# Input projection of a hybrid encoder block: 512-column token-major products, and q, k, v of two heads accumulated while x arrives

## The chip, the cores and the metric

The kernel runs on one core of a Trainium2 chip. The metric is the device time of one launch in microseconds (us). TensorE (PE) multiplies, VectorE (DVE), ScalarE (ACT) and GpSimd (POOL) do elementwise work, and DMA queues move data between DRAM, the on-chip SBUF and, by the engines, PSUM, where TensorE accumulates. P is 128.

## The reference, cut to what matters

One layer on x of 1024 tokens by 1024 features, all fp32. The change concerns the first lines, the input projection of 3104 columns, and what feeds on it.

```python
h = rms_norm(x, norm_mix)                     # x * rsqrt(mean(x*x) + eps) * gain
proj = h @ w_in                               # 1024 x 3104
q, k, v, z, b_f, b_b, a_f, a_b, su, sv = split(proj, [512, 512, 512, 512, 8, 8, 8, 8, 512, 512])
qkv = silu(short_conv(concat(q, k, v), conv_w))           # 5 taps along the tokens
o_a = bidir_gated_deltanet(qkv, z, b_f, b_b, a_f, a_b)    # 8 heads of 64, chunks of 64 tokens, two directions
o_b = spatial_gating(su, sv)                  # gelu, rms norm of v, a 128x128 mix of the tokens of a chunk, u * mix, rms norm
x = x + concat(o_a, o_b) @ w_out
x = rms_norm(x + square(relu(rms_norm(x) @ w_ff1)) @ w_ff2)
```

The rms factor of a token (1/rms) is one number per token. The kernel multiplies with the gain-scaled x and applies the factor to the products.

## The kernel before

*Precision.* Each fp32 operand is split into a rounded part and a remainder (xh and xl, w[:, 0] and w[:, 1]), and `mm3` makes one product from three matmuls (L140 to L142): first high by high, then the two cross terms. A `PE` line L140 in the profile is thus any large product; the tiles tell which.

*First stage (`first`).* For each of the 8 slices dt of 128 features, x comes transposed (xT, 512 KB), ACT and DVE make xh and xl, and eight blocks of 128 tokens accumulate 288 columns in eight PSUM banks: half of z and the 32 gate columns. Then x is read a second time, token by token (xtok), and ACT sums its squares (L241). POOL raises to the power -0.5 (`rsqrt`, L134 and L135). The result per token, rstd, is transposed on TensorE (L250) and written to DRAM as rs_d (L253), and read back over all partitions as rrow (L254): channel-major products, which have tokens along the columns, need a row.

*Projection (`project`).* Items follow each other in the order "01z23abcd". A digit is a head pair: q, k and v, each 128 channels by two halves of 512 tokens, with w stationary and x moving (channel-major). z is the other half of z, and a to d are the four gating groups, with x stationary and 256 columns of w moving (token-major, `tok_mm`). An item's weights are loaded while the one ahead runs: SP reads 512 KB into raw, ACT casts it (L148), POOL subtracts (L149). There are three such w buffers and two raw buffers.

*After an item.* A channel-major half is multiplied by rrow on DVE into cx (L330); then come the five-tap convolution on DVE and ACT (L422 to L428), turns to token order on TensorE (L450), the products of chunks (`stage1`: L548 in 64x64 tiles), an inversion of 32x32 triangles on DVE (L579, L581; L589 and L591 transpose its result into V and VT), and products of 32x32 tiles (L599, L611, L612). Decay factors are made by L517. The token-major parts go through ACT (gelu L337, silu L265) to `sgu`, which mixes four token blocks of one group at a time.

*Order.* `run` is a planner: each step is a generator that yields its cost ("pe 2.6 act 1" means 2.6 us of PE and 1 of ACT), lanes ("conv", "chunk0", "sgu", ...) queue such steps, and a lane's step is put in front of the projection's next when the planner's clocks of the engines say that it is ready by then. The clocks begin at the values of `self.t.update(dve=2.0, act=4.0, pool=3.0)`. What it gives out is one program; a scheduler then orders each engine's queue, where chunk, scan and convolution steps carry a priority. Engines run their queues in order.

*Then* come the scan (L743 to L810) with the out-projection, and the MLP of 3072 matmuls of 512 columns.

Of the kernel before, what the change touches and what calls it, by code (L numbers as in the profile page):

```python
# [10 lines left out]
F32 = mybir.dt.float32  # L11
# [8 lines left out]
P = 128  # L20
S = 1024
# [32 lines left out]
class Kern:  # L54
# [149 lines left out]
    def tok_mm(self, ps, b, w, dts):  # L204

        tb = slice(b * P, (b + 1) * P)
        for dt in dts:
            wd = w[dt // 4]
            self.mm3(ps, self.xh[dt][:, tb], self.xl[dt][:, tb], wd[:, 0, dt % 4], wd[:, 1, dt % 4],
                     dt == 0, dt == NT - 1)  # L210

    def first(self, xp):

        nc, a, tkx, tkp = self.nc, self.a, self.tkx, self.tkp
        N = 288
# [3 lines left out]
        acc = [self.psd() for _ in range(3)] + [self.psg() for _ in range(5)]  # L219
        two = [tkx.tile([P, 2, S], F32, tag=k, name="xraw") for k in ("n", "A")]  # L220
        one = lambda: self.rawp.tile([P, S], F32, tag="raw", name="xraw")
        w = []
        for dt in range(NT):
            if dt in (0, 1, 4, 7):
                k = 1 if dt in (0, 7) else 3
                pool, tag = {0: (self.wp, "w"), 1: (self.wp, "w"), 4: (tkx, "cm"), 7: (tkp, "lane")}[dt]
                raw = self.cvp.tile([P, k, N], F32, tag="ca", name="raw", bufs=2)
                t = self.load_w(a["wz1"][:, dt:dt + k], raw, pool.tile([P, 2, k, N], F32R, tag=tag, name="w"), nc.gpsimd)
                w += [t[:, :, i] for i in range(k)]
            self.load_x(dt, xp, two[dt // 2 - 1][:, dt % 2] if 2 <= dt < 6 else one())  # L230
            if dt == 0:
                self.late_consts()
            for b in range(NB):
                tb = slice(b * P, (b + 1) * P)
                self.mm3(acc[b][:, :N], self.xh[dt][:, tb], self.xl[dt][:, tb], w[dt][:, 0], w[dt][:, 1],
                         dt == 0, dt == NT - 1)
        for b in range(NB):
            xr = (tkx, "tok") if b % 2 else (self.cvp, "cx")
            xr = xr[0].tile([P, D], F32, tag=xr[1], name="xtok", bufs=2)
            nc.sync.dma_start(xr, a["x"][b])  # L240
            nc.scalar.activation(xr, xr, AF.Square, accum_out=ss[:, b:b + 1])  # L241
        self.w0 = self.load_in(a["wqkv"][0], [NT, P])
        raw = tkp.tile([P, 3, N], F32, tag="nod", name="raw")
        for b in range(3):
            (nc.scalar.copy if b == 1 else nc.vector.tensor_copy)(raw[:, b], acc[b][:, :N])
            acc[b] = raw[:, b]
        with self.tc.high_priority(offset=400):
            self.rsqrt(self.rstd, ss, 1.0 / D)
# [5 lines left out]
            nc.sync.dma_start(self.rrow, self.rs_d.partition_broadcast(P))  # L254
        gt = tmp[:, 0:256].rearrange("p (b c) -> p b c", b=NB)
        for b in range(NB):
            nc.vector.tensor_scalar(gt[:, b], acc[b][:, 256:288], self.rstd[:, b:b + 1], None, ALU.mult)
            self.evac_z(acc[b], b, 1)
        return gt, tmp, sml

    def evac_z(self, ps, b, h):
        nc = self.nc
        if b % 4 == 0:
            self.zt = self.sgup.tile([P, 4, 256], F32, tag="uv", name="zt", bufs=3)
        nc.scalar.activation(self.zt[:, b % 4], ps[:, 0:256], AF.Silu, scale=self.rstd[:, b:b + 1])  # L265
        if b % 4 == 3:
            nc.sync.dma_start(self.z_d[b - 3:b + 1, :, h * 256:h * 256 + 256].rearrange("b t c -> t b c"), self.zt)

    def project(self):
# [3 lines left out]
        qkv = lambda p: [("q", p, j) for j in range(3)]  # L273
        items = []
        for c in "01z23abcd":
            items += qkv(int(c)) if c.isdigit() else [("z", 0, 0)] if c == "z" else [("s", "abcd".index(c), 0)]

        def load(kind, p, j):
            if kind == "q":
                return self.load_in(self.a["wqkv"][p * 3 + j], [NT, P])  # L280
            return [self.load_in(self.a["ws"][p, h] if kind == "s" else self.a["wz0"][h], [4, 256]) for h in range(2)]
# [6 lines left out]
        w = self.w0  # L288
        for it, (kind, p, j) in enumerate(items):
            nxt = None  # L290
            if kind == "q":
                n = p * 3 + j - 2
                yield lambda: n < 0 or n in self.taps
                for h in range(2):
                    yield "pe 2.6" + (" act 1 pool 2.3" if h else "")
                    if h == 0:
                        x = self.cvp.tile([P, S + 4], F32, tag="cx", name="cx", bufs=2)
                        nc.gpsimd.memset(x[:, 0:2], 0.0)
                        nc.gpsimd.memset(x[:, S + 2:S + 4], 0.0)
                    else:  # L300
                        nxt = load(*items[it + 1])
                    ps = self.psd()
                    th = slice(h * 512, h * 512 + 512)
                    for dt in range(NT):
                        if dt == NT // 2:
                            yield "pe 2.6 dve .6"
                        self.mm3(ps, w[:, 0, dt], w[:, 1, dt], self.xh[dt][:, th], self.xl[dt][:, th],
# [3 lines left out]
            else:  # L311
                for h in range(2):
                    if kind == "s":
                        yield lambda: self.uv > 0
                    for i in range(4):
                        yield "pe 2.6 act .4" + (" act 1 pool 2.3" if h and i == 1 else "")
                        if i == 0 and kind == "s":
                            self.uv -= 1
                            uv = self.sgup.tile([P, 4, 256], F32, tag="uv", name="uv", bufs=3)
                        if h and i == 1 and it + 1 < len(items):  # L320
                            nxt = load(*items[it + 1])
                        ps = self.psd()
                        self.tok_mm(ps[:, :256], h * 4 + i, w, range(NT))
                        late.append((self.evac_sgu, ps, uv, i, p, h) if kind == "s" else (self.evac_z, ps, h * 4 + i, 0))
                        flush(1)
# [9 lines left out]
    def evac_sgu(self, ps, uv, i, g, h):  # L335
        b = h * 4 + i
# [873 lines left out]
```

## Time and profile before

| what | us |
| --- | --- |
| median of 3 runs (lowest, highest) | 1381.99 (1380.45, 1386.76) |
| the profiled execution | 1388.61 |
| its span on the core | 1386.6 |
| PE busy / DVE / ACT / POOL | 1333.1 / 734.8 / 499.8 / 255.1 |
| first stage, projection, scan and out-projection, MLP | to 37.6, to 412, to 687, to the end |

The span is what the trace covers; 2.0 us of the execution lie around it. Shares of busy time are averages over stages. A matmul's busy time is modelled, so its pitch, the distance from start to start in a stretch, says more than its mean duration. PEclk is the clock that was granted to TensorE, as a share of the full one.

### The profile page before, as it was taken

What the parts mean: (1) busy time and instruction counts of PE and PEld (TensorE: products, weight loads), DVE (VectorE), ACT (ScalarE), POOL (GpSimd) and SP (SyncE); (2) the same over time, 40 slices, a digit from 0 to 9 for tenths busy, and PEclk for the clock granted to TensorE, in tenths of its full rate; (3) what the DMA queues carried; (4) which work ended last, traced back from release to release, by engine and by line L of the source; (5) the groups of instructions that cost most, each with busy time, mean ns of one, the idle gap of its engine ahead of it and who ended that gap; (6) DMA issues with size and microseconds to landing.
All of it is one profiled execution on the core that took longest, in us unless ns stands there. A gap on an engine that the chain in (4) does not pass through costs nothing.

```text
span 1386.6 us, 21359 instructions
## 1 busy us (share of the span) xinstructions
PE 1333.1 (96%) x8606; PEld 1124.1 (81%) x8606; DVE 734.8 (53%) x1201; ACT 499.8 (36%) x924; POOL 255.1 (18%) x330
## 2 busy tenths in 40 slices
PE   7899999999987999998999999999999999999997
PEld 7677876889987898876788888888888888888885
DVE  3579677976664566686543433434334343343345
ACT  5565443574545663411531311312113121131224
POOL 2232212233365875100000000000000000000013
PEclk9999899989989999999999999999999999999999
DMA  9622232235235563320012102121021210212103
GB/s 335 246 97 109 93 85 78 85 100 160 80 65 138 131 158 80 117 77 1 1 54 69 42 12 69 54 69 38 16 69 54 69 38 16 69 54 69 36 18 129
DMA packets 125617, 113.55 MB, mean 82 GB/s; under 512 B 75048, under 2 KB 98736, under 8 KB 124976
## 3 DMA queue, kind: packets, MB, share of 16 engines
q1 hardware_dynamic: 124368, 110.10, 25.4%
q10 hardware_dynamic: 1152, 2.10, 0.4%
q8 instruction: 68, 1.11, 0.3%
q14 instruction: 29, 0.24, 0.1%
HBM read 85.42 MB, written 27.33 MB: 81 GB/s over the span
## 4 chain that ended last, share of the span: by engine, by line
PE 78%; DVE 11%; ACT 3%; POOL 2%; issue 2%; DMA 2%; SPq 1%; POOLq 0%; ACTq 0%; DVEq 0%
PE psd L140 14%; PE psd L141 14%; PE psd L142 13%; PE psg L140 9%; PE psg L141 9%; PE psg L142 9%; PE psg L752 3%; DVE lt L579 2%; DVE lane L581 2%; PE psg L548 2%; PE psg L743 2%; PE pss L797 1%; DVE ca L425 1%; DVE cm L425 1%; PE psg L599 1%
## 5 line engine op out<-in xcount | busy, mean ns | idle before, releaser
L140 PE MATMUL psg<-fh,w 128*128 128x512 f32 x512 | 199.3, 389 | 0.6 <-DVE fl L964 0.6
L142 PE MATMUL psd<-w,ff 128*128 128x512 f32 x512 | 199.3, 389 | 0.0
L141 PE MATMUL psd<-w,ff 128*128 128x512 f32 x512 | 199.2, 389 | 0.0
L141 PE MATMUL psg<-fl,w 128*128 128x512 f32 x512 | 199.1, 389 | 0.0
L142 PE MATMUL psg<-fh,w 128*128 128x512 f32 x512 | 198.0, 389 | 0.0
L148 ACT CAST w<-raw 128x512 fp32r<-128x512 f32 (+3 forms) x122 | 98.8, 811 | 268.7 <-PE psd L142 150.0
L140 PE MATMUL psd<-w,ff 128*128 128x512 f32 x512 | 195.3, 389 | 0.0
L1038 DVE SCALAR_TENSOR_TENSOR x<-psd,r,x 128x512 f32<-128x512 f32 x128 | 94.5, 749 | 170.0 <-PE psd L142 169.9
L149 DVE TENSOR_TENSOR w<-raw,w 128x512 fp32r<-128x512 f32 (+1 forms) x96 | 83.4, 870 | 103.7 <-ACT w L148 101.8
L996 POOL TENSOR_SCALAR fs<-fs 128x1 f32<-128x1 f32 x8 | 5.5, 693 | 671.8 <-ACT scr L993 671.8
L1021 ACT ACTIVATE relu<-psg 128x512 f32<-128x512 f32 x64 | 38.1, 595 | 244.7 <-PE psg L142 244.7
L140 PEld LDWEIGHTS psg<-fh,w 128*128 128x128 f32 x512 | 96.1, 188 | 20.8 <-DVE fl L964 0.8
L140 PEld LDWEIGHTS psd<-w,ff 128*128 128x128 f32 x512 | 96.1, 188 | 20.3 <-DVE x L1038 0.4
L141 PEld LDWEIGHTS psd<-w,ff 128*128 128x128 f32 x512 | 96.2, 188 | 20.0
L142 PEld LDWEIGHTS psg<-fh,w 128*128 128x128 f32 x512 | 96.1, 188 | 20.0
L141 PEld LDWEIGHTS psg<-fl,w 128*128 128x128 f32 x512 | 96.1, 188 | 19.9
L142 PEld LDWEIGHTS psd<-w,ff 128*128 128x128 f32 x512 | 96.1, 188 | 20.0
L140 PE MATMUL psd<-w,xh 128*128 128x256 f32 (+1 forms) x344 | 104.0, 305 | 7.9 <-ACT xh L199 7.9
L1022 DVE TENSOR_TENSOR relu<-relu 128x512 f32<-128x512 f32 x64 | 44.2, 690 | 115.1 <-ACT relu L1021 115.1
L141 PE MATMUL psd<-w,xh 128*128 128x256 f32 (+1 forms) x344 | 102.8, 302 | 0.0
L142 PE MATMUL psd<-w,xl 128*128 128x256 f32 (+1 forms) x344 | 101.6, 301 | 0.0
L140 PE MATMUL psd<-xh,w 128*128 128x512 f32 x192 | 77.6, 404 | 3.0 <-DVE cx L330 2.6
(229 smaller groups left out, 2523.0 us busy)
## 6 DMA issues: line engine op xcount, KB each, us to landing
raw<-in_w SPq DMA_DIRECT2D x32, 512.0 KB, 3.6
raw<-in_w SPq DMA_DIRECT2D x64, 256.0 KB, 2.5
raw<-in_wqkv SPq DMA_DIRECT2D x12, 512.0 KB, 3.5
tok_d<-tok SPq DMA_DIRECT2D x12, 512.0 KB, 4.7
xtok<-in_x SPq DMA_DIRECT2D x8, 512.0 KB
t_d<-zero SPq DMA_DIRECT2D x8, 512.0 KB, 7.6
a_d<-A SPq DMA_DIRECT2D x4, 1024.0 KB, 3.9
raw<-in_ws SPq DMA_DIRECT2D x8, 512.0 KB, 3.5
```

Source lines behind the costliest of these rows:

```text
L140: mm(ps, lh, rh, start=start, stop=False)
L141: mm(ps, lh, rl, start=False, stop=False)
L142: mm(ps, ll, rh, start=False, stop=stop)
L148: nc.scalar.copy(w[:, 0], raw)
L149: lo.tensor_tensor(w[:, 1], raw, w[:, 0].bitcast(F32), ALU.subtract)
L425: nc.vector.scalar_tensor_tensor(acc, x[:, t:t + S], cw[:, t:t + 1], acc, ALU.mult, ALU.add)
L548: nc.tensor.matmul(ps[c * 64:c * 64 + 64, b * 64:b * 64 + 64], cm[1][hs, ch], cm[w][hs, ch], start=True, stop=True)
L579: nc.vector.tensor_tensor(tv, X[:, k:k + 1, 0:k].broadcast_to([P, m, k]), X[:, k + 1:32, k:k + 1].broadcast_to([P, m, k]), ALU.mult)
L752: nc.tensor.matmul(ps[:, (r * 2 + t) * P:(r * 2 + t + 1) * P], l[:, r, t], uw[:, r, t], start=True, stop=True)
L1021: nc.scalar.activation(r, pf, AF.Relu)
L1022: nc.vector.tensor_tensor(r, r, r, ALU.mult)
L1038: nc.vector.scalar_tensor_tensor(x1[b][:, ns], pf, r4[:, b:b + 1], x1[b][:, ns], ALU.mult, ALU.add)
```

## The change

- The first stage accumulates q, k and v of head pair 0 (six banks of 512 columns, channel-major, 18 matmuls for each dt) and the gates alone (one bank, 32 columns for a token block, L253 after). Its weights w0 are 416 columns wide: three times 128 and 32.
- x is not read again: ACT squares the xT slices, DVE adds them up, and eight matmuls against a column of ones (L258) give the sums per token. rstd (L262) is laid on diagonals (dg) on DVE, and two matmuls of ones by dg (L270) give rrow in PSUM, which ACT copies. rs_d is gone.
- z is one item of 512 columns, and the gating groups go two at a time, 256 columns of u and 256 of v: order "z1a23b". `sgu` works on two token blocks of two groups instead of four blocks of one.
- Weights come in pieces of 512 columns with nine buffers. Those of the first stage are made as before. Of the others ACT writes the rounded part and its negative, and a DMA from POOL's queue adds the fp32 weights onto the negative (`accum_op`, L164).
- The squares of q, k and of sgu go to a PSUM tile; the token-order tile `tok` is one tile of two halves with a write for each half; one convolution buffer is moved (cax); the planner's clocks begin at dve=0, act=6.

The diff, cut to its core:

```diff
-    def load_in(self, src, shape):
-        raw = self.rawp.tile([P] + shape, F32, tag="raw", name="raw")
-        w = self.wp.tile([P, 2] + shape, F32R, tag="w", name="w")
-        return self.load_w(src, raw, w, self.nc.gpsimd)
+    def piece(self, src, n=512, early=False):
+
+
+        nc = self.nc
+        raw = self.rawp.tile([P, 512], F32, tag="raw", name="raw")[:, :n]
+        w = self.wp.tile([P, 2, 512], F32R, tag="w", name="w")
+        if early:
+            self.load_w(src, raw, w[:, :, :n], nc.gpsimd)
+        else:
+            nc.sync.dma_start(raw, src)
+            nc.scalar.copy(w[:, 0, :n], raw)
+            nc.scalar.mul(w[:, 1, :n], raw, -1.0)
+            nc.gpsimd.dma_start(w[:, 1, :n], src, accum_op=ALU.add)
+        return w
...
+            w.append(self.piece(a["w0"][dt], N, True))
+            self.load_x(dt, xp, xraw[dt])
+            pool, tag = (tkx, "cax") if dt % 2 else (self.cvp, "ca")
+            sq = sqs if dt == 0 else pool.tile([P, S], F32, tag=tag, name="sq")
+            nc.scalar.activation(sq, xraw[dt], AF.Square)
+            if dt:
+                nc.vector.tensor_tensor(sqs, sqs, sq, ALU.add)
...
+        self.w0 = [self.piece(a["wt"][0, dt]) for dt in range(NT)]
+        for dt in range(NT):
+            for i in range(6):
+                j, h = divmod(i, 2)
+                ws, th = slice(j * P, j * P + P), slice(h * 512, h * 512 + 512)
+                self.mm3(qkv[i], w[dt][:, 0, ws], w[dt][:, 1, ws], self.xh[dt][:, th], self.xl[dt][:, th],
+                         dt == 0, dt == NT - 1)
             for b in range(NB):
-                tb = slice(b * P, (b + 1) * P)
-                self.mm3(acc[b][:, :N], self.xh[dt][:, tb], self.xl[dt][:, tb], w[dt][:, 0], w[dt][:, 1],
-                         dt == 0, dt == NT - 1)
-        for b in range(NB):
-            xr = (tkx, "tok") if b % 2 else (self.cvp, "cx")
-            xr = xr[0].tile([P, D], F32, tag=xr[1], name="xtok", bufs=2)
-            nc.sync.dma_start(xr, a["x"][b])
-            nc.scalar.activation(xr, xr, AF.Square, accum_out=ss[:, b:b + 1])
-        self.w0 = self.load_in(a["wqkv"][0], [NT, P])
-        raw = tkp.tile([P, 3, N], F32, tag="nod", name="raw")
-        for b in range(3):
-            (nc.scalar.copy if b == 1 else nc.vector.tensor_copy)(raw[:, b], acc[b][:, :N])
-            acc[b] = raw[:, b]
-        with self.tc.high_priority(offset=400):
-            self.rsqrt(self.rstd, ss, 1.0 / D)
-            rst = self.psd()
-            nc.tensor.transpose(rst[:NB, :P], self.rstd, self.ident)
-            rsr = sml[:NB, 128:256]
-            nc.vector.tensor_copy(rsr, rst[:NB, :P])
-            nc.sync.dma_start(self.rs_d.rearrange("(b t) -> b t", t=P), rsr)
-            nc.sync.dma_start(self.rrow, self.rs_d.partition_broadcast(P))
+                tb, gs = slice(b * P, (b + 1) * P), slice(3 * P, N)
+                ps = gate[:, b * 32:b * 32 + 32]
+                for i, (x, k) in enumerate(((self.xh, 0), (self.xh, 1), (self.xl, 0))):
+                    nc.tensor.matmul(ps, x[dt][:, tb], w[dt][:, k, gs], start=dt == b == i == 0, stop=dt == NT - 1 and i == 2,
+                                     skip_group_check=True)
+            if dt == NT - 3:
+
+                for b in range(NB):
+                    nc.tensor.matmul(gate[:, 256 + b:257 + b], sqs[:, b * P:(b + 1) * P], ones[:, 0:1],
+                                     start=False, stop=True, skip_group_check=True)
+                with self.tc.high_priority(offset=400):
+                    nc.vector.tensor_scalar(ss, gate[:, 256:256 + NB], 1.0 / D, EPS, ALU.mult, ALU.add)
+                    nc.gpsimd.tensor_tensor(self.rstd, ss, self.mhalf.broadcast_to([P, NB]), ALU.pow)
+
+                    dg = self.sgup.tile([P, NB, P], F32, tag="uv", name="dg", bufs=3)
+                    nc.vector.tensor_tensor(dg, self.ident.unsqueeze(1).broadcast_to([P, NB, P]),
+                                            self.rstd.unsqueeze(2).broadcast_to([P, NB, P]), ALU.mult)
+            if dt == NT - 2:
+                with self.tc.high_priority(offset=100):
+                    for h in range(2):
+                        nc.tensor.matmul(misc, ones, dg[:, h * 4:h * 4 + 4].rearrange("p b t -> p (b t)"),
+                                         start=True, stop=True)
+                        nc.scalar.copy(self.rrow[:, h * 512:h * 512 + 512], misc)
...
-        for c in "01z23abcd":
...
+        for c in "z1a23b":
...
+            for _ in range(min(n, len(todo))):
+                nxt.append(self.piece(todo.pop(0)))
...
+                    ps = self.psd()
+                    tb = slice(b * P, (b + 1) * P)
+                    for dt in range(NT):
+                        if dt % 4 == 0:
+                            yield "pe 2.7 act .3" + (" act 1.2" if b >= 6 and dt == 0 and todo else "")
+                        if b >= 6 and dt == 0:
+                            load(1)
+                        self.mm3(ps, self.xh[dt][:, tb], self.xl[dt][:, tb], w[dt][:, 0], w[dt][:, 1], dt == 0, dt == NT - 1)
...
-                sq = self.sgup.tile([P, 512], F32, tag="sj", name="sq")
+                sq = self.psg()
...
-        nc.sync.dma_start(self.tok_d[p, j], tok.rearrange("p b c -> p (b c)"))
+            nc.sync.dma_start(self.tok_d[p, j][:, h * 512:h * 512 + 512], tok)
...
-        self.mm3(pm, ws[:, 0, g], ws[:, 1, g], vs[:, 0].rearrange("p b c -> p (b c)"),
-                 vs[:, 1].rearrange("p b c -> p (b c)"), True, True)
+        for g in range(2):
+            self.mm3(pm[:, g * 256:g * 256 + 256], ws[:, 0, k * 2 + g], ws[:, 1, k * 2 + g], vh[:, :, gs[g]],
+                     vl[:, :, gs[g]], True, True)
...
-        self.wp = self.pool("wp", 3, right, **R)
+        self.wp = self.pool("wp", 9, right, **R)
...
-        self.t.update(dve=2.0, act=4.0, pool=3.0)
+        self.t.update(dve=0.0, act=6.0, pool=3.0)
```

What it moves on the engines, at three places. On TensorE in the projection, the products of a chunk (`stage1`, 64x64 tiles; L548 before, L590 after) stood one by one between the 256-column products of z. Before:

```order
L548 MATMUL psg<-ca 64x64 x25
L140 MATMUL psd<-w,xh_227 128x256
L548 MATMUL psg<-ca 64x64
L141 MATMUL psd<-w,xh_227 128x256
L548 MATMUL psg<-ca 64x64
L142 MATMUL psd<-w,xl_228 128x256
L548 MATMUL psg<-ca 64x64
L140 MATMUL psd<-w,xh_261 128x256
```

After, pair 0's stand among pair 1's 512-column products:

```order
L559 MATMUL psg<-dr_650,dl 128x512 x3
L590 MATMUL psg<-ca,cm 64x64 x16
L590 MATMUL psg<-cm 64x64 x2
L493 MATMUL psg<-cst,cm 128x128 x4
L590 MATMUL psg<-cm 64x64 x14
L140 MATMUL psd<-xh_201,w 128x512
L141 MATMUL psd<-xl_202,w 128x512
L142 MATMUL psd<-xh_201,w 128x512
```

They now stand in blocks. (The number behind ` x` is a count; a row's tile names are output<-inputs.) Up to the first product of the scan, TensorE goes to 64x64 tiles and back 64 times before and 15 times after, to 32x32 tiles 17 and 18 times; after, 17 times it goes from 32x32 to 64x64 tiles, where pair 1's L653 and L654 (L611 and L612 before) alternate with L590.

On TensorE in the first stage, in the stretch of one dt. Before:

```order
L140 MATMUL psd<-w,xh_169 128x288 x3
L140 MATMUL psg<-w,xh_169 128x288 x5
L141 MATMUL psd<-w,xh_169 128x288 x3
L141 MATMUL psg<-w,xh_169 128x288 x5
L142 MATMUL psd<-w,xl_170 128x288 x3
L142 MATMUL psg<-w,xl_170 128x288 x5
```

After, a part of one dt:

```order
L140 MATMUL psg<-xh_175,w 128x512
L141 MATMUL psg<-xl_176,w 128x512
L142 MATMUL psg<-xh_175,w 128x512
L253 MATMUL psg<-w,xh_175 128x32 x2
L253 MATMUL psg<-w,xl_176 128x32
L253 MATMUL psg<-w,xh_175 128x32 x2
L253 MATMUL psg<-w,xl_176 128x32
```

24 products of 288 columns have become 18 of 512 and 24 of 32.

On POOL, from the first weights to the first qkv item's. Before:

```order
L149 TENSOR_TENSOR w<-raw,w 128x1024
L298 MEMSET cx 128x2
L299 MEMSET cx 128x2
L134 TENSOR_SCALAR sml<-sml 128x8
L135 TENSOR_TENSOR rstd<-sml,mhalf 128x8
L149 TENSOR_TENSOR sgw<-raw,sgw 128x512
L495 MEMSET zero 128x1024
L149 TENSOR_TENSOR w<-raw,w 128x1024 x2
```

After:

```order
L149 TENSOR_TENSOR w<-raw,w 128x416 x8
L164 DMA w<-in_wt 128x512 x7
L262 TENSOR_TENSOR rstd<-sml,mhalf 128x8
L149 TENSOR_TENSOR sgw<-raw,sgw 128x512
L164 DMA w<-in_wt 128x512
L164 DMA w<-in_wqkv 128x512
L537 MEMSET zero 128x1024
```

The subtractions of whole items have become DMA issues, and seven of them, for z's weights, stand ahead of rstd.

More of the change, by code (lines that the diff above doesn't have):

```diff
@@ L218, in first @@
         ss = sml[:, 0:NB]
-        acc = [self.psd() for _ in range(3)] + [self.psg() for _ in range(5)]
-        two = [tkx.tile([P, 2, S], F32, tag=k, name="xraw") for k in ("n", "A")]
-        one = lambda: self.rawp.tile([P, S], F32, tag="raw", name="xraw")
+        qkv = [self.psd(), self.psd()]
+        misc = self.psd()
+        qkv += [self.psg() for _ in range(4)]
+        gate = self.psg()
+        two = [tkx.tile([P, 2, S], F32, tag=k, name="xraw") for k in ("n", "A", "cm")]
+        xraw = [t[:, i] for t in two for i in range(2)] + [tkp.tile([P, S], F32, tag=k, name="xraw") for k in ("lane", "nod")]
@@ L222, in first @@
+        ones = self.sgup.tile([P, P], F32, tag="sm", name="ones", bufs=2)
+        nc.vector.memset(ones, 1.0)
+        sqs = self.sgup.tile([P, S], F32, tag="uv", name="sqs", bufs=3)
         w = []
         for dt in range(NT):
[L224 to L229, printed above, removed]
@@ L262, in evac_z @@
         nc = self.nc
[L263 to L267, printed above, removed]
+        if b % 2 == 0:
+            self.zt = self.sgup.tile([P, 2, 512], F32, tag="uv", name="zt", bufs=3)
+        nc.scalar.activation(self.zt[:, b % 2], ps, AF.Silu, scale=self.rstd[:, b:b + 1])
@@ L269, in project, with new_cx, third @@
+        if b % 2:
+            nc.sync.dma_start(self.z_d[b - 1:b + 1].rearrange("b t c -> t b c"), self.zt)
+    def new_cx(self):
+        x = self.cvp.tile([P, S + 4], F32, tag="cx", name="cx", bufs=2)
+        self.nc.gpsimd.memset(x[:, 0:2], 0.0)
+        self.nc.gpsimd.memset(x[:, S + 2:S + 4], 0.0)
+        return x
+    def third(self):
+        yield "dve 1.4"
+        x = self.new_cx()
+        for h in range(2):
+            self.evac_qkv(self.qkv0[4 + h], x, h, 0, 2)
     def project(self):
@@ L286, in flush, with load @@
                 f(*args)
-        w = self.w0
+        for j in range(2):
+            yield "dve 1.4"
+            x = self.new_cx()
+            for h in range(2):
+                self.evac_qkv(self.qkv0[j * 2 + h], x, h, 0, j)
+        self.side("conv", self.third())
+        w, todo = self.w0, []
+        def load(n):
+            for _ in range(min(n, len(todo))):
+                nxt.append(self.piece(todo.pop(0)))
         for it, (kind, p, j) in enumerate(items):
-            nxt = None
+            nxt = []
+            after = loads(*items[it + 1]) if it + 1 < len(items) else []
             if kind == "q":
@@ L293, in project @@
                 yield lambda: n < 0 or n in self.taps
+                todo = after
                 for h in range(2):
-                    yield "pe 2.6" + (" act 1 pool 2.3" if h else "")
+                    yield "pe 2.6" + (" act 2.4" if todo else "")
+                    load(4 - h)
                     if h == 0:
[L297 to L301, printed above, removed]
+                        x = self.new_cx()
                     ps = self.psd()
@@ L311, in project @@
             else:
-                for h in range(2):
-                    if kind == "s":
-                        yield lambda: self.uv > 0
[L315 to L325, printed above, removed]
+                load(len(todo))
+                w += nxt
+                nxt, todo = [], after
+                for b in range(NB):
+                    if kind != "z" and b % 2 == 0:
+                        yield lambda: self.uv > 0
+                        self.uv -= 1
+                        uv = self.sgup.tile([P, 2, 512], F32, tag="uv", name="uv", bufs=3)
+                    ps = self.psd()
[6 more added lines that the diff above has]
+                        self.mm3(ps, self.xh[dt][:, tb], self.xl[dt][:, tb], w[dt][:, 0], w[dt][:, 1], dt == 0, dt == NT - 1)
+                    late.append((self.evac_z, ps, b) if kind == "z" else (self.evac_sgu, ps, uv, b, "ab".index(kind)))
+                    flush(1)
             w = nxt
@@ L444, in heads @@
             yield "pe .5 " + ("act 1.1 dve .6" if j < 2 else "dve .7")
-            if h == 0:
-                tok = self.tkx.tile([P, NB, P], F32, tag="tok", name="tok", bufs=2)
-                self.opened += 1
+            tok = self.tok[:, h]
             pt = self.psg()
@@ L492, in zeros @@
     def zeros(self):
-        z = self.sgup.tile([P, 4, 256], F32, tag="uv", name="zero", bufs=3)
+        z = self.sgup.tile([P, 2, 512], F32, tag="uv", name="zero", bufs=3)
         self.nc.gpsimd.memset(z, 0.0)
@@ L889, in outproj @@
         t = [tkx.tile([P, 2, D], F32, tag=k, name="x1") for k in ("cm", "n", "A")]
-        self.x1 = [t[b // 2][:, b % 2] for b in range(6)] + [tkx.tile([P, D], F32, tag="tok", name="x1", bufs=2) for _ in range(2)]
+        self.x1 = [t[b // 2][:, b % 2] for b in range(6)] + [tkx.tile([P, D], F32, tag=k, name="x1") for k in ("tok", "cax")]
         for b in range(NB):
@@ L1046, in scratch @@
         self.z_d = dp.tile([NB, P, 512], F32, name="z_d")
-        self.rs_d = dp.tile([S], F32, name="rs_d")
         self.cg_d = dp.tile([2, 16, 2, 2, 8, 64], F32, name="cg_d")
```

103 lines of the change are left out of this document (50 added, 53 removed).

## The prediction

> **What bounds the kernel now.** I read the page first (busy shares, slices, the chain that ended last), then TensorE in four stretches, then its waits and its timeline.
>
> ```profile
> span 1386.6 us, 21359 instructions
> PE 1333.1 (96%) x8606; PEld 1124.1 (81%) x8606; DVE 734.8 (53%) x1201; ACT 499.8 (36%) x924; POOL 255.1 (18%) x330
> ...
> PEclk9999899989989999999999999999999999999999
> ...
> PE 78%; DVE 11%; ACT 3%; POOL 2%; issue 2%; DMA 2%; SPq 1%; POOLq 0%; ACTq 0%; DVEq 0%
> ```
>
> ```profile
> 0.00:37.60 37.60, 29.61 (x193) 0.95 0.90 318
> 37.60:412.00 374.40, 355.54 (x3210) 0.93 0.34 109
> 412.00:687.00 275.00, 257.90 (x2179) 0.98 0.34 90
> 687.00:1386.00 699.00, 690.01 (x3042) 1.00 0.15 52
> ```
>
> The columns after a stretch's length are TensorE's busy time with its instructions, its granted clock, the DMA share and GB/s. TensorE is the bound throughout. The MLP (last row) runs at full clock with 9 us of idle time and isn't edited. The projection (second row) has 374.4 - 355.5 = 18.9 us of idle time and a clock of 0.93, worth up to 0.07 x 374.4 = 26 us. Busy time is not work here, though: a matmul that waits for the array counts as busy. That shows in the timeline, where 64x64 products alternate with wide ones (columns: start, duration, line, shapes, count):
>
> ```profile
> 128.58 0.34 PE L548 MATMUL psg<-ca 64*64 64x64 f32 x6
> 128.85 0.38 PE L140 MATMUL psd<-w,xh 128*128 128x256 f32 x1
> 129.17 0.32 PE L548 MATMUL psg<-ca 64*64 64x64 f32 x2
> 129.42 0.38 PE L141 MATMUL psd<-w,xh 128*128 128x256 f32 x1
> ...
> 219.32 0.50 PE L142 MATMUL psd<-xh,w 128*128 128x512 f32 x1
> 219.76 0.33 PE L548 MATMUL psg<-cm,ca 64*64 64x64 f32 x2
> 220.01 0.50 PE L140 MATMUL psd<-xh,w 128*128 128x512 f32 x1
> ```
>
> One wide and two small take 129.42 - 128.85 = 0.57 us, or 220.01 - 219.32 = 0.69. The pitches of undisturbed stretches come from windows (the first busy column is TensorE):
>
> ```profile
> 18.21:34.16 15.95, 15.95 (x123) 15.95 (x122) 5.74 (x4) 10.73 (x16) 4.00 (x5) 1.00 1.03 383
> 71.73:89.10 17.37, 17.37 (x78) 14.36 (x77) 14.57 (x12) 6.48 (x9) 6.73 (x6) 1.00 0.30 90
> 160.47:169.18 8.71, 8.71 (x76) 8.71 (x74) 5.17 (x13) 6.07 (x8) 4.05 (x6) 1.00 0.16 63
> ```
>
> The order has 76 matmuls of 512 columns in the second and 72 of 256 in the third (the rest overlap its edges): 0.2286 and 0.121 us each. The first has about 120 of 288 columns: 0.1325. The small ones cost 0.27/6 = 0.045 at most, so one round trip between tile sizes costs 0.57 - 0.12 - 0.09 = 0.36 us and 0.69 - 0.23 - 0.09 = 0.37 us. The Trainium skill ("TensorEngine Tiling (Array Packing)", Key Properties) says that changing the tiling mode drains TensorE; it gives no price, and these rows agree with the rule. The clock falls in just such stretches, of small or alternating products:
>
> ```profile
> 130.00:150.00 20.00, 20.00 (x78) 0.57 0.20 80
> 400.00:412.00 12.00, 11.14 (x234) 0.61 0.54 105
> ```
>
> **The change, part by part.** *First stage.* Before: 192 matmuls of 288 columns and one transpose, 37.6 us. After: 18 x 8 = 144 of 512 columns, 144 x 0.2286 = 32.9 us, and 192 gate products of 32 columns, each with its own 128-column weight load. No row has these; the nearest are 64 columns wide:
>
> ```profile
> 64.69 0.55 PE L377 MATMUL psg<-tmp,sums 128*128 128x64 f32 x4
> 65.08 1.05 PE L381 MATMUL psg<-tmp,sums 128*128 128x64 f32 x8
> 65.94 0.48 PE L141 MATMUL psd<-xl,w 128*128 128x512 f32 x1
> ```
>
> (65.94 - 65.08)/8 = 0.108 us, so 192 x 0.108 = 20.6 us; the lower bound is the 0.045 above (8.6 us), the upper the 0.1325 of 288 columns (25.4 us). I take 20.6, since the width is nearest. The eight ones-matmuls for the sums add 8 x 0.108 = 0.9 us, and the two plain fp32 ones of 512 columns 2 x 8 x 0.108 = 1.7, an estimate that scales those 64 columns by eight. The start, 37.6 - 29.6 = 8.0 us of idle time, and some 4 us of slow first matmuls (29.6 against 192 x 0.1325 = 25.4) stay. 56.1 + 8 + 4 = 68 us at most, 64 if the wait for data in the middle is covered by longer matmuls; I take 66: **+28 us**.
>
> *Projection columns.* Before, after the first stage: 576 matmuls of 512 columns (131.7 us) and 960 of 256 (116.2 us). After: 432 + 576 of 512, 1008 x 0.2286 = 230.4 us. **-17.5 us**. With the first stage, **+10.5**: the wider columns save 12 us and the gates, no longer part of a wide matmul, cost about 20.
>
> *Tile-size trips.* Counted in the two orders up to the first scan product: before 64 trips between 128 and 64 and 17 between 128 and 32; after 15 and 18, and 17 between 64 and 32, since L590's blocks stand together. 81 x 0.37 = 30 us before; after 33 x 0.37 = 12, and 17 for 0 to 6 (nothing in the trace shows a 32/64 trip; I take 3). **-15 us** (-12 to -18).
>
> *The rms row.* Before, L253 and L254 write and read it through DRAM behind 4 MB of zeros, and x is read a second time (8 x 512 KB).
>
> ```profile
> 45.82 0.45 SPq L498 DMA_DIRECT2D t_d<-zero  x1
> ...
> 48.66 1.14 SPq L254 DMA_DIRECT2D rrow<-rs_d  x1
> 49.84 7.80 SPq L498 DMA_DIRECT2D t_d<-zero  x6
> ```
>
> ```profile
> PE psg L599 <- DVE VT L591: 5.2, 2, 4.4
> PE psd L140 <- DVE cx L330: 2.6, 1, 2.6
> ...
> PE psd L142 <- POOL w L149: 1.7, 1, 1.7
> ```
>
> In this list of TensorE's waits (total, times, longest), the row's lateness costs 2.6 us and the POOL subtraction 1.7 us; both go. Late next is the pair-0 evacuation (L330, six at 0.685 us on DVE) and the last z weights, which get a buffer only when TensorE frees it; 2 us come back.
>
> ```profile
> L330 DVE TENSOR_TENSOR cx<-psd,rrow 128x512 f32<-128x512 f32 x24 | 16.2, 685 | 4.2 <-PE psd L142 4.2
> ```
>
> L599's waits for DVE's transposes stay: the DVE work of a pair is the same. I take idle **-5 us**: 18.9 to 14 (5 to 25).
>
> *Clock.* The worst interleaved stretch (130 to 150 at 0.57, 20 x 0.43 = 8.6 us) has no successor in the new order; the transposes at 400 to 412 (12 x 0.39 = 4.7 us) have. 26 to 14: **-12 us** (0 to -20).
>
> *Weights.* The subtractions leave POOL (22 x 2.61 us), and a second ACT pass and 42 accumulating DMAs from POOL's queue come instead.
>
> ```profile
> L148 ACT CAST w<-raw 128x1024 fp32r<-128x1024 f32 x22 | 22.9, 1043 | 25.5 <-PE psd L142 24.3 <-issue 0.5 <-DMA raw<-in_wqkv 0.3
> ...
> L659 ACT CAST vs<-uv 128x512 fp32r<-128x512 f32 x7 | 4.3, 615 | 0.9 <-PE psg L142 0.8
> ...
> L149 POOL TENSOR_TENSOR w<-raw,w 128x1024 fp32r<-128x1024 f32 x22 | 57.2, 2610 | 61.6 <-ACT w L148 61.6
> ...
> raw<-in_w SPq DMA_DIRECT2D x64, 256.0 KB, 2.5
> ...
> t_d<-zero SPq DMA_DIRECT2D x8, 512.0 KB, 7.6
> ```
>
> ACT: 42 x 2 x 0.615 = 51.7 us against 22.9; at 36% busy it is hidden, unless an evacuation stands behind it. The accumulating DMA has no row: 2.5 us is the fastest 256 KB, 7.6 us a transfer in a full queue. I take 2.5 to 4 because DMA is 34% used in that stretch. A qkv item's second piece gets its buffer at the last z block's first matmul, 23 x 0.229 = 5.3 us before the item, and is read 12 x 0.229 = 2.7 us into it: 8.0 us, less 1.2 for ACT, leaves 6.8 us for the transfer. At 4 it is hidden, at 7.6 not. Behind it on POOL stand the q/k norms and rstd, which wait with it.
>
> *Moved items.* z and gating groups 0 and 1 now run ahead of pairs 2 and 3. Their SP writes (z_d, sg_d) go with them and have readers only after the scan; 12 writes of tok become 24, 12 x 0.45 us more of SP's issue time by the t_d row above, ahead of raw loads that have a whole item's time (5.5 us for a half). Evacuations of 512 columns on ACT replace pairs of 256, under TensorE's 24 x 0.229 us. The sum of squares takes a PSUM buffer in place of one in SBUF, of the five (tag g) that the transposes use too; 0, at most a wait of one DVE reduction. No term.
>
> *Scan part.* Trips are 63 before, 59 after; pair 3's transposes now fall into it, and 42 instead of 21 out-projection matmuls lie ahead of the final L867, which waited 5.3 us:
>
> ```profile
> PE psg L772 <- ACT S L763: 7.2, 1, 7.2
> PE psg L867 <- DVE oacc L844: 5.3, 1, 5.3
> ```
>
> 21 x 0.229 = 4.8 us cover most of it; pair 3's lateness gives some 3 us back: **-2 us** (-8 to +12). The 7.2 us bubble stays.
>
> Sum: +10.5 - 15 - 5 - 12 - 2 = -23.5. The profiled run took 1388.6 us (its span and 2.0 around it), 6.6 above the median 1382.0 of the runs: 1365 on its own basis, **1358** for a median.
>
> **Rivals.** *Losses all but vanish:* after's blocks keep the clock at full and DVE ahead; idle 5 and clock loss 3 instead of 14 and 14: 20 us more, 1338. For it: DVE is 53% busy. Against: L591's wait was DVE's and DVE's work per pair doesn't shrink.
>
> *Clock and idle stay as they are* (26 and 19): only trips and columns count, 10.5 - 15 - 2 = -6.5, 1375, no change within measurement.
>
> *Slower: the accumulating DMAs come late.* Eleven items start behind a piece. If a piece takes 10 us instead of under 6.8, TensorE waits 3.2 us each, 35 us: 1393. It decides from (23.5 + 6.8)/11 = 2.8 us of wait each to slow it by 0.5%, so from 9.6 us a transfer. For it: POOL and DVE hinder each other here,
>
> ```profile
> 49.42 2.28 DVE L369 TENSOR_SCALAR tmp<-tmp 128x128 f32<-128x128 f32 x1 [4.35 <-ACT tmp L357]
> ...
> 49.26 4.71 POOL L149 TENSOR_TENSOR w<-raw,w 128x1024 fp32r<-128x1024 f32 x2 [4.80 <-ACT w L148]
> ```
>
> 2.28 us for 128 columns while POOL works, against 0.69 for L330's 512. Against: a queue at a third of its share, and DVE's long instructions between. The Trainium skill ("SBUF — State Buffer", "The "DVE blocks DMA" trap") says that a DMA issued from GpSimd gets no descriptors written while DVE holds the shared ports, 3100 ns for a 620 ns transfer; by that 2.5 us more per piece, an estimate, would still be hidden. No run here has such a DMA yet.
>
> **Chances.** Forecast 0.48 (1343 to 1372), losses vanish 0.18 (1320 to 1343), losses stay 0.14 (1372 to 1386), late DMAs 0.16 (1389 to 1420), a scan part that gives it all back 0.04. The gate products' bounds move each case by -12 to +5. Range 1322 to 1393; the forecast's own is 1343 to 1372. A measurement tells 0.5% (7 us) from no change: faster (under 1375) 0.48 + 0.18 + 0.02 = 0.68, same 0.14, slower 0.18.
>
> **What would show it.** The first q item's start at 64 to 68 us after 192 gate products at a pitch near 0.108; the first scan product 20 to 28 us before 412; 512-column pitches of 0.2286 in the token-major items; the clock of that stretch at 0.95 or more; no wait of TensorE for a DMA into w. I am wrong if the gates cost much less than 0.1, if TensorE's list of waits is led by w or by DVE's transposes ahead of L641, or if the scan part exceeds 287 us.

## The result: 1.4% slower

Median 1402.27 us (1399.65 to 1404.48, 4 runs) against 1382.56 us of the kernel before beside it: a ratio of 1.0138, 95% interval 1.0107 to 1.0169. A second comparison (e5 below) gave 1.0135 (1.0077 to 1.0192). The profiled execution took 1403.32 us.

The page of the changed kernel: TensorE as busy as before, DVE with less to do, and a new queue (software_dynamic) for the accumulating DMAs.

```profile
span 1401.6 us, 20830 instructions
...
PE 1344.9 (96%) x8265; PEld 1119.0 (80%) x8265; DVE 715.7 (51%) x1209; ACT 518.2 (37%) x960; POOL 247.6 (18%) x353
...
PEclk9999899997979899999999999999999999999999
...
q0 software_dynamic: 6048, 11.01, 4.9%
```

Stretches of TensorE (length, busy time, clock, DMA share, GB/s), cut at the end of the first stage, at the last projection product and at the MLP's start. Of the kernel before:

```profile
37.60:394.90 357.30, 342.84 (x2966) 0.94 0.34 110
394.90:687.00 292.10, 270.60 (x2409) 0.96 0.34 89
```

and of the changed one:

```profile
68.00:394.80 326.80, 311.67 (x2324) 0.93 0.49 130
394.80:702.60 307.80, 282.32 (x2552) 0.94 0.36 93
```

The first stage is 68.0 - 37.6 = 30.4 us longer and the projection behind it 30.5 us shorter, so that both kernels are through with it at 395 us. The 15 us between the two traces are lost after that, 307.8 against 292.1 us. (By the medians it is 20 us: the profiled execution of the kernel before was 6.6 us above its median, that of the changed one 1.1.) Idle time in the projection is 15.1 us (14.5 before) and the clock 0.93 (0.94): neither got better.

The gate products came as sized. 24 of them take 68.02 - 65.43 = 2.59 us, 0.108 each (timeline of TensorE; first and last rows):

```profile
65.43 0.29 PE L253 MATMUL psg<-w,xh 128*128 128x32 f32 x2
65.56 0.26 PE L253 MATMUL psg<-w,xl 128*128 128x32 f32 x1
...
68.02 0.47 PE L140 MATMUL psd<-w,xh 128*128 128x512 f32 x1
```

TensorE's longest waits between 68 and 395 us (total, times, longest) are for ACT and DVE, as they were before, and hardly any is for a weight. Those for VT, which led before with 5.2 us in all (4.4 of them behind 395 us), are 2.1 up to the MLP:

```profile
PE psg L493 <- ACT n L560: 3.7, 1, 3.7
PE psg L559 <- ACT n L560: 2.8, 1, 2.8
PE psg L641 <- DVE VT L633: 2.1, 1, 2.1
...
PE psd L142 <- DMA w<-in_wqkv: 0.2, 1, 0.2
```

### The profile page after: what moved, and what is told of

It reads as the page before. It is cut to its first block, busy times and chain, and to the rows that moved or that the text cites. A ratio compares the mean times of both kernels' runs of the same rounds, so it can differ in the third digit from the quotient of the medians.

```text
span 1401.6 us, 20830 instructions
## 1 busy us (share of the span) xinstructions
PE 1344.9 (96%) x8265; PEld 1119.0 (80%) x8265; DVE 715.7 (51%) x1209; ACT 518.2 (37%) x960; POOL 247.6 (18%) x353
## 4 chain that ended last, share of the span: by engine, by line
PE 60%; DVE 2%; POOL 1%; DMA 1%; ACT 1%; issue 1%; SPq 1%; POOLq 0%; ACTq 0%; DVEq 0%
PE psd L140 10%; PE psd L142 10%; PE psd L141 10%; PE psg L140 8%; PE psg L142 8%; PE psg L141 8%; PE psg L801 2%; PE psg L792 1%; PE psg L859 1%; PE pss L846 1%; PE psg L916 0%; DVE x L963 0%; DMA t_d<-off 0%; ACT scr L1042 0%; PE psg L1010 0%
## 5 line engine op out<-in xcount | busy, mean ns | idle before, releaser
L148 ACT CAST w<-raw 128x512 fp32r<-128x512 f32 (+2 forms) x104 | 77.3, 745 | 237.6 <-PE psd L142 125.6
L140 PE MATMUL psd<-w,xh 128*128 128x512 f32 x192 | 78.0, 407 | 0.0
L141 PE MATMUL psd<-w,xh 128*128 128x512 f32 x192 | 77.9, 406 | 0.0
L142 PE MATMUL psd<-w,xl 128*128 128x512 f32 x192 | 77.8, 405 | 0.0
L140 PE MATMUL psd<-xh,w 128*128 128x512 f32 x160 | 66.5, 416 | 6.2 <-ACT xh L209 6.2
```

Source lines behind the costliest of these rows:

```text
L140: mm(ps, lh, rh, start=start, stop=False)
L141: mm(ps, lh, rl, start=False, stop=False)
L142: mm(ps, ll, rh, start=False, stop=stop)
L148: nc.scalar.copy(w[:, 0], raw)
```

## The experiments

Times are medians; a ratio is to the kernel before on the same chip, with its interval. Unless said otherwise 0.001 is 1.4 us.

### Order, gates and weights, one by one

**e1.** `for c in "z1a23b"` becomes `"1z23ab"`, with pair 1's first pieces as w0.

> The changed kernel with its items in the order 1 z 2 3 a b instead of z 1 a 2 3 b, so that the last pair's q, k, v are projected 43.9 us earlier. Theory A (the order gives the gain back: pair 3's inversion on DVE ends inside the scan, whose part takes 307.8 us instead of 292.1): the scan part comes back to 290 to 295 us and the time falls by 12 to 20 us, to 1382 to 1390. Theory B (the first stage, 30.4 us longer, is the loss and the order of the rest is indifferent): 1399 to 1405.

1.0178 (1.0106 to 1.0250), 1413.22 us, slower than either theory had. Theory A saw one half: from the first scan product to the MLP it takes 709.3 - 433.9 = 275 us instead of 300. But the scan starts 31 us later, since TensorE now waits for the gating groups (vs of ACT 11.6 us, of POOL 7.5) and for weights (11.3). The order moved the loss.

**e2.** In the kernel before: `"01z23abcd"` becomes `"0z1ab23cd"`.

> The kernel before with only its items reordered: 0 z 1 a b 2 3 c d instead of 0 1 z 2 3 a b c d, which is the order of the changed kernel. Theory A: the last pair's chain falls into the scan here too, slower by 10 to 20 us (1392 to 1402). Theory B: within 5 us of the kernel before.

1.0721 (1.0648 to 1.0794), 1488.60 us: a hundred microseconds, which no theory had. The new order has 128 trips between 128 and 64 (64 before), 72 between 128 and 32 (17) and 13 between 64 and 32. Two long stretches look like this (the window of TensorE, then its timeline):

```profile
374.00:394.00 20.00, 20.00 (x72) 0.50 0.00 1
```

```profile
379.89 0.47 PE L548 MATMUL psg<-cm 64*64 64x64 f32 x2
380.29 0.58 PE L142 MATMUL psd<-w,xl 128*128 128x256 f32 x1
380.80 0.47 PE L548 MATMUL psg<-cm 64*64 64x64 f32 x2
```

TensorE counts as busy for all of 20 us, at a clock of 0.50, and one round trip takes 380.80 - 379.89 = 0.91 us for 0.2 us of products. The same alternation had begun at 360.72 us at a clock of 1.00, where a round trip took 361.55 - 360.98 = 0.57 us; after some 4.5 us of it the clock was at 0.50 (windows of TensorE):

```profile
360.70:365.20 4.50, 4.50 (x25) 1.00 0.00 0
365.60:374.00 8.40, 8.40 (x31) 0.50 0.00 0
```

132 more trips for 102 us are 0.77 us each: about twice the price at full clock, with all else that the order moved in it.

**e3.** The gates' loop runs over `(self.xh, 0)` alone.

> The changed kernel without the two cross products of the gates: 64 matmuls of 32 columns in the first stage instead of 192 (the gates lose precision, nothing else changes). By the pitch of 0.108 us 128 x 0.108 = 13.8 us go from the first stage. Theory B: all of it arrives at the end, 1386 to 1390. Theory A: the first stage is shorter by 13.8 too, but DVE is what the pairs wait for, so that less than half arrives, 1394 to 1402.

1.0094 (1.0060 to 1.0128), 1400.39 us, 6 us better than the changed kernel; by the two intervals between none and 12. Not all of the 13.8 us arrive, and whether any do is open.

**e4.** `if early:` becomes `if True:`.

> The changed kernel with the remainders of all weights made by POOL's subtraction, as before, instead of the accumulating DMAs from POOL's queue (42 x 1.29 us more on POOL, 42 x 0.6 us less on ACT). Theory C (the accumulating DMAs are the loss): faster by 8 us or more. Theories A and B: no faster, 1400 to 1412, since TensorE waits 0.2 us in all for such a DMA.

1.0166 (1.0092 to 1.0240), 1410.77 us, no faster. Theory C falls: with TensorE's 0.2 us of waits for these DMAs above, they are not the loss.

**e8.** Both halves of a piece on POOL:

```diff
-            nc.scalar.copy(w[:, 0, :n], raw)
-            nc.scalar.mul(w[:, 1, :n], raw, -1.0)
-            nc.gpsimd.dma_start(w[:, 1, :n], src, accum_op=ALU.add)
+            lo = w[:, 1, :n]
+            nc.gpsimd.tensor_copy(w[:, 0, :n], raw)
+            nc.gpsimd.tensor_tensor(lo, raw, w[:, 0, :n].bitcast(F32), ALU.subtract)
```

> The changed kernel with both halves of a weight piece made on POOL (cast and subtraction), none on ACT and without accumulating DMAs: 42 x 1.2 us and 13.5 us of waits for loads go from ACT. Theory E: TensorE's waits for ACT (L493 for n, L559 for n, L801 for uw: 12.5 us) shrink by half or more and the time falls by 8 to 20 us. Theory D: no faster, or slower, since POOL gets 42 x 2.6 us.

1.0176 (1.0127 to 1.0225), 1411.59 us. ACT no longer waits for loads (13.5 us in the changed kernel), and nothing is gained: theory E falls. **e5**, the changed kernel beside it, is the 1.0135 above.

> The changed kernel itself, unedited, beside the next three on one chip, so that they can be compared with it there. All theories: 1.010 to 1.017 times the kernel before.

### The trips: one number in both kernels

**e6, e7.** `URGENT = dict(chunk=100, ...)` becomes `chunk=200`, in the changed kernel and in the one before.

> The changed kernel with the priority of the chunk steps raised from 100 to 200. In the projection the trips between tile sizes fall from 15 to 8 (128 and 64), from 18 to 6 (128 and 32) and from 17 to 0 (32 and 64); no work is changed. Theory D (tile-size trips with the low clock in them cost 0.4 to 0.9 us each): 33 trips less, faster by 10 to 20 us. Theory E (a weight piece's cast waits on ACT for its load, with PSUM evacuations behind it, and the trips are only where TensorE happens to be when it waits): within 6 us of the changed kernel.

> The kernel before with the same number, 100 to 200: its trips fall from 64 to 9 and from 17 to 9. Theory D: 63 trips less, by the 0.37 us of the prediction 23 us, with the low clock of those stretches up to 45: 1338 to 1362. Theory E: within 8 us of the kernel before, since the trips fill time in which TensorE would wait for DVE.

e7: 0.9832 (0.9787 to 0.9878), 1364.92 us; 63 trips less for 23 us are 0.37 us each, and nothing more came from the low clock, for which theory D allowed up to 45. e6: 1.0044 (1.0017 to 1.0071), 1392.79 us; by the counts in its expectation (15, 18 and 17 to 8, 6 and none) 36 trips are gone, not 33, and 12.6 us are 0.35 each. So theory E falls: fewer trips are faster in both. The price is that of the whole edit, though: the priority also moves products, and TensorE's waits for VT rise with it, from 5.2 to 10.4 us in e7 and from 2.1 to 14.8 in e6. e7 is already faster than either kernel. At nearly equal trips (14 and 18) the changed kernel is 1.0044 - 0.9832 = 0.021, 29 us, slower. In e6 one wait leads:

```profile
PE psg L641 <- DVE VT L633: 14.8, 2, 14.2
```

### DVE's inversions

**e9, e10.** In e6 and e7, the 60 instructions of the loop are left out in each of pairs 2 and 3 (`if p > 1: continue` behind the loop's yield); what follows works on uninverted triangles.

> The changed kernel with priority 200 and without the 60 DVE instructions of the inversion in pairs 2 and 3 (L621 and L623, 22 us of DVE per pair; what follows then works on uninverted triangles, TensorE's work is the same). Theory F (with the projection done sooner on TensorE, DVE is what the last two pairs wait for): TensorE's 14.8 us of waits for VT go and pair 3's products no longer fall into the scan; 20 us or more faster than the run with priority 200 (ratio 0.990 or less against 1.0044). Theory G (the first stage's longer products are the loss, DVE is beside the path): within 8 us of it.

> The kernel before with priority 200 and the same 60 instructions left out (L579 and L581 in pairs 2 and 3). Theory F: it waited 10.4 us for VT at one place, so 8 to 14 us faster than with priority 200 alone (0.975 against 0.983), and the distance to the run above shrinks from 28 us to about the 10 us that the counts of matmuls give. Theory G: 0 to 10 us faster, and the distance stays 20 us or more.

e9: 0.9897 (0.9859 to 0.9934), 20 us faster than e6. e10: 0.9819 (0.9797 to 0.9840), 2 us faster than e7: theory F had 8 to 14, theory G up to 10. The distance shrinks from 29 to 11 us, as theory F had it; theory G wanted 20 or more left. The 14.8 us of waits for VT are 1.8 in e9:

```profile
PE psg L641 <- DVE VT L633: 1.8, 1, 1.8
```

So with the priority at 200 the inversions of pairs 2 and 3 are worth 20 us in the changed kernel and 2 in the one before, with the same DVE work.

**e11.** e9 with the gates' one product.

> The first of these (priority 200, no inversion in pairs 2 and 3) and also without the two cross products of the gates: 64 instead of 192 matmuls of 32 columns. Theory F: with DVE out of the way the 13.8 us of gate products arrive at the end, 10 to 16 us faster than the first. Theory G says the same of the gates; if less than 7 us arrive, something else than DVE paces the pairs.

0.9910 (0.9880 to 0.9939), 1371.58 us: nothing arrives, against theory F. Its profile shows where TensorE stops instead:

```profile
PE psg L141 <- POOL vs L706: 7.1, 1, 7.1
PE psd L140 <- ACT uv L382: 5.9, 1, 5.9
PE psg L821 <- ACT S L812: 5.2, 1, 5.2
```

**e12.** e6 with the order `"z123ab"`.

> The changed kernel with priority 200 and its items in the order z 1 2 3 a b instead of z 1 a 2 3 b; nothing is left out. Theory F: DVE gets the last pair's q, k, v 43.9 us sooner, so that pair 3's chain ends ahead of the scan: 8 to 20 us faster than with priority 200 alone (ratio 0.990 to 0.999). Theory H (the order only moves the loss, as the first reordering did: 3 pairs in a row starve TensorE behind DVE's convolutions): within 6 us of it or slower.

0.9990 (0.9970 to 1.0010), 1382.05 us, 7 us better than e6: theory F's ratio is just met, its 8 us just missed.

### Why DVE comes late

Start of an inversion's first or last step (tiles of 30 columns, timeline of DVE): pair 0's first, pair 1's last, pair 2's first. Before:

```profile
115.40 2.38 DVE L579 TENSOR_TENSOR lt<-lane 128x30 f32<-128x30 f32 x1
...
266.04 0.22 DVE L579 TENSOR_TENSOR lt<-lane 128x30 f32<-128x30 f32 x1
...
288.55 0.19 DVE L579 TENSOR_TENSOR lt<-lane 128x30 f32<-128x30 f32 x1
```

The changed kernel:

```profile
166.34 0.18 DVE L621 TENSOR_TENSOR lt<-lane 128x30 f32<-128x30 f32 x1
...
293.69 0.21 DVE L621 TENSOR_TENSOR lt<-lane 128x30 f32<-128x30 f32 x1
...
346.31 0.18 DVE L621 TENSOR_TENSOR lt<-lane 128x30 f32<-128x30 f32 x1
```

Pair 0's starts 51 us later, and between pairs 1 and 2 lie 52.6 us instead of 22.5. By 160 us DVE had done 43 us of work instead of 90 (windows of DVE; the changed kernel, then before):

```profile
40.00:160.00 120.00, 43.29 (x63) 0.93 0.61 164
```

```profile
40.00:160.00 120.00, 90.38 (x134) 0.93 0.38 138
```

Its longest wait in there is for pair 0's first squares (L500 of ACT):

```profile
124.98 0.69 DVE L501 TENSOR_REDUCE nrm<-psg 128x8 f32<-128x512 f32 x1 [24.64 <-ACT psg L500]
```

ACT makes them from L498, which copies the token turn (L493) that TensorE does only when z is through, right behind the decay product L559:

```profile
116.60 0.40 PE L559 MATMUL psg<-dr,dl 96*128 96x512 f32 x1
116.83 0.60 PE L493 MATMUL psg<-cst,ca 128*128 128x128 f32 x4
```

The convolved q was done by 79 us. In the program, L559's PSUM tile is asked for just ahead of L493's.

**e13.** e6 with the decay products asked for later:

```diff
-        yield "lat 4"
+        yield "lat 16" if p == 0 else "lat 4"
```

> The changed kernel with priority 200, and the planner's wait ahead of pair 0's decay products (L559) raised from 4 to 16 us. Its PSUM tile stands ahead of those of pair 0's turns (L493), so that these no longer wait for z's end: they stand 22 and 54 matmuls sooner. No work is changed. Theory F1 (DVE's idle 25 us at 100 to 125 come from these turns): DVE does 15 us or more beyond the 43 us of the changed kernel by 160 us, and the time falls by 8 us or more against priority 200 alone (1.0044). Theory F2 (they come from z's 44 us, in which DVE has no other pair to work on): DVE's work by 160 us rises by under 8 us, the time stays within 6 us.

0.9826 (0.9781 to 0.9871), 1363.83 us: 30 us less than e6, with no work changed. The time is F1's, but not its measure, since DVE's work by 160 us rose by 8 us only. Trips don't explain it: TensorE's timeline up to the scan has 17 of them, 14 in e6. Pair 0's inversion starts at 153.57 us (168.70 in e6), pair 2's at 309.77 (338.02), and of e6's waits for VT (14.8 us) and vs (9.0 of ACT) none is left. TensorE's idle time from 68 to 703 us falls from 57.8 to 31.5 us, 26 of the 30 (windows of TensorE; e6, then e13):

```profile
68.00:703.00 635.00, 577.25 (x4939) 0.95 0.43 112
```

```profile
68.00:703.00 635.00, 603.47 (x5045) 0.97 0.44 115
```

**e14, e15.** e13 with the orders `"1z23ab"` and `"z123ab"`.

> The same with the items in the order 1 z 2 3 a b: pair 1's q, k, v are projected ahead of z. Theory F2: DVE gets pair 1's convolutions 44 us sooner, does 20 us or more beyond the changed kernel's 43 by 160 us, and the time falls by 10 us or more against priority 200 alone, to 0.997 or less. Theory F1: no better than the run above. Theory H (order only moves the loss to the gating groups at the end, as in the first reordering): 1.004 or more.

> The same as the first with the order z 1 2 3 a b. Theory F1: 0.993 or less (the 0.999 of that order without it, less 8 us). Theory F2: 0.996 to 1.002, as without it, since z still comes first.

e14: 1.0091 (1.0056 to 1.0126), 1398.93 us: DVE does 12.5 us more by 160 us than the changed kernel, and the time is worse (TensorE waits 15.3 us for weights, 11.0 for vs, 7.6 for VT), so F2 falls and H is borne out. e15: 0.9895 (0.9860 to 0.9931), 1372.48 us, as F1 had it (0.993 or less).

**e16.** The changed kernel with `lat 16` alone, priority 100.

> The changed kernel with the planner's wait ahead of pair 0's decay products at 16 us and the priority left at 100. Its trips between tile sizes are 11 and 14, and none between 32 and 64 (15, 18 and 17 in the changed kernel). Theory F1 (the held-back start of pair 0 is what turned the change into a loss): the 30 us that it gave at priority 200, less some for trips that remain, so 0.985 to 0.998 of the kernel before, no longer slower. If it needs the higher priority: 1.005 or more.

0.9850 (0.9782 to 0.9917), 1366.74 us. One number turns 1.4% slower into 1.5% faster. Its turns stand ahead:

```profile
99.50 0.60 PE L493 MATMUL psg<-cst,ca 128*128 128x128 f32 x4
```

```profile
101.57 0.69 DVE L501 TENSOR_REDUCE nrm<-psg 128x8 f32<-128x512 f32 x1 [1.28 <-ACT psg L500]
...
154.68 0.19 DVE L621 TENSOR_TENSOR lt<-lane 128x30 f32<-128x30 f32 x1
...
282.65 0.20 DVE L621 TENSOR_TENSOR lt<-lane 128x30 f32<-128x30 f32 x1
...
312.13 0.19 DVE L621 TENSOR_TENSOR lt<-lane 128x30 f32<-128x30 f32 x1
```

Pair 0's inversion starts 12 us sooner, and the gap between pairs 1 and 2 is 29.5 us instead of 52.6: by 35 us pair 2 is ahead, and the traces differ by 39. The second half of that is a matter of order too. In the changed kernel no token turn of pair 2 stands on TensorE between 226 and 299 us; they come behind pair 1's L641, which waits for pair 1's inversion. In e16 they stand at 255, 261 and 268 us, and pair 2's 64x64 products at 273 to 281, ahead of L641 at 289. Besides, no trip between 32 and 64 is left, and 8 others less. On TensorE the same time shows as 10 us less idle time and a clock of 0.97 instead of 0.94 from 68 to 703 us, which is worth 0.03 x 635 = 19 us, an estimate (the changed kernel, then e16):

```profile
68.00:703.00 635.00, 594.38 (x4876) 0.94 0.42 112
```

```profile
68.00:703.00 635.00, 604.48 (x5052) 0.97 0.43 115
```

So at priority 100 the late inversions cost little in waits for VT (2.1 us); trips and the clock go with them, and e16 alone doesn't part these. e13 against e6 does better, with nearly as many trips (17 and 14).

**e17.** e7 with `lat 16`.

> The kernel before with priority 200 and the same wait of 16 us. Its pair 0 was not held back (its inversion starts at 117 us), so theory F1 gives no gain here: within 5 us of 0.983. If the number is simply better for the planner whatever the kernel: 0.975 or less.

0.9789 (0.9734 to 0.9845), 1360.49 us, the fastest with the whole computation. By the ratio it is 6 us below e7, just outside the 5 that F1 allowed, with intervals that overlap: the wait is worth 30 us and more in the changed kernel and little or nothing in the one before.

**e18.** e13 with the gates' one product.

> The changed kernel with priority 200, the wait of 16 us, and without the two cross products of the gates (64 instead of 192 matmuls of 32 columns). If TensorE paces the projection now that DVE is fed sooner, 10 us or more of the 13.8 arrive (0.975 or less); if DVE or ACT still pace it, under 6 us (0.979 or more).

0.9779 (0.9722 to 0.9837), 1358.12 us: 6.5 us of 13.8, between the two expectations, with intervals that overlap e13's. How much of the gates' 20 us is on the path stays open.

## Why the prediction was wrong, step by step

It forecast 1358 us, 24 faster; measured were 1402, 20 slower. The rival that ended on that side, late accumulating DMAs, isn't the cause. What came is two others at once: clock and idle time stayed as they were (0.14), and the scan part took more than the gain (0.04).

- *First stage, +28:* +30.4, right; the gates' pitch of 0.108 us is exact.
- *Columns, -17.5:* right as far as the pitch shows. In the z item 75 matmuls of 512 columns follow each other from 75.87 to 92.87 us, 0.227 each.
- *Trips, -15:* 0.37 us forecast; 0.37 (e7) and 0.35 (e6) by the priorities, with all that these move. The Trainium skill's rule ("TensorEngine Tiling (Array Packing)", Key Properties), that a change of mode drains TensorE, agrees with these prices. The 17 between 32 and 64 were mis-sized: 3 us taken, and four round trips take 313.30 - 311.59 = 1.71 us, 0.43 each, 7 us in all, so -11 instead of -15. The two priorities differ by 23.3 - 12.6 = 10.7 us.

```profile
311.59 0.33 PE L590 MATMUL psg<-cm,ca 64*64 64x64 f32 x2
311.85 0.24 PE L654 MATMUL psg<-yt,V 32*32 32x32 f32 x2
312.02 0.32 PE L590 MATMUL psg<-cm,ca 64*64 64x64 f32 x2
...
313.30 0.27 PE L590 MATMUL psg<-cm,ca 64*64 64x64 f32 x1
```

- *Idle, -5, and clock, -12:* nothing came (idle 15.1 us against 14.5, clock 0.93 against 0.94), and this is the first failed step. "L599's waits for DVE's transposes stay: the DVE work of a pair is the same" took the amount of DVE's work for its place in time: the inversions are the same, and pair 0's starts 51 us later, pair 2's 58. The waits for VT themselves fell from 5.2 to 2.1 us; those for ACT's n rose from 2.2 to 6.5. With the products in blocks (e6) the lateness shows as 14.8 us of waits for VT.
- *Scan part, -2:* +15.7, the second failed step. "Pair 3's lateness gives some 3 us back" priced products that fall into it, not the chain ahead of them: the last product of 32x32 tiles ends at 475 us instead of 413.
- *The signs:* "The first scan product 20 to 28 us before 412" took the end of the last chunk products for the start of the scan, which was at 395.4 us; now it is at 402.5. The scan part's 287 us were exceeded (300 from the first scan product on), and the clock's 0.95 was missed.
- *Late accumulating DMAs (0.16):* 4.6 us from issue to landing against 3.1 on SP's queue, as the listing of transfers shows, and TensorE waited 0.2 us for them. The 6.8 us of slack held. The Trainium skill ("SBUF — State Buffer", "The "DVE blocks DMA" trap") lets such a DMA wait for its descriptors while DVE holds the shared ports; 1.5 us more than SP's could be that or POOL's own issue, and no run here tells them apart.

```profile
raw<-in_wt SPq DMA_DIRECT2D x24, 256.0 KB, 3.1
w<-in_wt POOLq DMA_DIRECT2D x24, 256.0 KB, 4.6
```

By the stages of the two traces the misses are 2.4 us in the first stage, 19.0 in the projection (-49.5 forecast, -30.5 measured) and 17.7 in the scan part, 39 us, which is what lies between the forecast of -23.5 and the traces' +15.0. The 44 us of the medians hold 5.5 more because the two profiled executions lie 6.6 and 1.1 us above theirs. Term by term the projection's misses (4 for trips, 6 for idle, 13 for the clock) are 23 us, more than its stage shows: the terms are not separate. By experiments: of the 29 us between e6 and e7, 18 go with the inversions of pairs 2 and 3 (e9, e10) and 11 stay; less the 10.7 by which the two priorities differ, the 29 are the 19 that were measured, which is arithmetic on the same ratios and no test. That the 11 us that stay are the +10.5 of the matmul counts is not shown, since e11 and e18 don't find the gates in full.

Shown is that the place of pair 0's decay products in the program decides the sign (e16). That it acts through the start of the inversions is borne out by e13 against e6 (17 and 14 trips, 30 us, no wait for VT left) and by e9; no run leaves the inversions out and moves the decay products too, so what else the new order brings isn't parted from it. That the PSUM tile is what held L493 back is argued from the order alone: neither priority moved L493 ahead of L559 (119.07 us in e6), a later request for L559's tile did (98.86 in e13). Why pair 2's turns then also move ahead of pair 1's L641 was not tried.

## What to carry to other kernels

When TensorE's work is reordered, list for the second-busiest engine when each link of its serial chain can start, not how busy it is: here the same DVE work, 51 us late at its start, cost about 18 us (e9 and e10), more than the 12 that the wide matmuls were to save. Count trips between tile sizes in the order and price them with the clock they bring; a priority that keeps small products in a block was worth 23 us in the old kernel for one number. After a restructuring, try the planner's few constants again before judging it: with a wait of 16 instead of 4 the changed kernel is 1.5% faster, and with blocks as well (e13) level with the old one with blocks (e7). Give the old kernel the same tries: with both numbers (e17) it has 0.9789 against e13's 0.9826, so that at equal settings no run shows a gain from the change; the old one with the wait alone was not run.

## What the runs showed of the hardware

In e2, one 256-column product that alternates with two of 64x64 ran at a granted clock of 1.00 for some 4.5 us and then at 0.50, in the window shown for all of 20 us, with TensorE shown as busy throughout: 0.91 us a round trip against 0.57 at full clock. In the changed kernel a DMA that POOL issues takes 0.88 us of POOL in the mean (L164) and landed 256 KB in 4.6 us, accumulating.
